# The prompt's attention with stationary values and streaming transposed weights, divided before the transpose

## The chip, the cores and the metric

The kernel runs on one core of a Trainium2 chip. The metric is device time in microseconds (us) of one execution; lower is better. A core has a matrix engine (TensorE, PE in the profile, with its weight loads as PEld), three engines for elementwise work (VectorE as DVE, ScalarE as ACT, GpSimd as POOL), a queue that issues most transfers (SyncE, SP) and 16 DMA engines. Matrix products read SBUF and write to PSUM; VectorE and ScalarE read PSUM.

## The reference

One layer of a streaming encoder runs for two request groups that share weights: one prompt of 256 tokens and eight sampled sequences of 16 tokens. A projection feeds an RWKV-7 recurrence and a sparse attention with 16 heads of 64; both are gated, mixed and projected, and an expert layer (PEER, 16384 experts) follows. The change touches the attention of the prompt, which is, cut to what matters:

```python
def block(args):
    qh, qih, wih, qp = args
    rel = jax.nn.relu(jnp.einsum('bqhd,bsd->bqhs', qih, ki_all))
    score = jnp.einsum('bqh,bqhs->bqs', wih, rel)
    adm = (qp[:, None] // CHUNK) >= k_chunk[None, :]
    score = jnp.where(adm[None], score, -jnp.inf)
    vals, idx = lax.top_k(score, topk)
    ok = vals > -jnp.inf
    ks = gather(k_all, idx)
    vs = gather(v_all, idx)
    s = jnp.einsum('bqhd,bqkhd->bhqk', qh, ks).astype(jnp.float32) * (dh ** -0.5)
    s = jnp.where(ok[:, None], s, -jnp.inf)
    p = jax.nn.softmax(s, axis=-1).astype(vs.dtype)
    return jnp.einsum('bhqk,bqkhd->bqhd', p, vs)
```

For a query, a head's output is the sum over keys of weight times value, with the weights divided by their sum. All data is float32.

## The kernel before

The kernel handles all 384 tokens (128 sampled, 256 of the prompt) in one pass. Its front part, up to about 730 us, is a string of units of five kinds, laid out in program order by the text `ORDER` (line 177): `R` is one pair of heads of the recurrence (`rwkv_pair`, eight of them), `D` one quarter of the attention (`dsa_quarter`, four heads, four of them), `G` a gate projection, `M` a piece of the modulation, `I` the index scores, and `1`, `2`, `3` the choice of keys. The mixing stage (`mix`, L1164) follows; it reads the recurrence's outputs back from memory (`parts`, L1155), and the attention's outputs for its second half. The expert layer takes the rest of the time.

Program order is not the order on the queues. The program is built with a planner, which simulates the units with its own prices, fixes each engine's queue order (so that projections of one unit stand between the steps of another), and hands buffers out as it goes. On the chip every engine runs its queue in order and waits at semaphores.

Projections multiply float32 data that is split in two rounded parts: ScalarE makes the high part `wh` (L230) and VectorE the low part `wl` (L234), and three products are added (tiles `mm<-...`). All matrix products pass the helper `mm` (L226); transposes carry their own lines.

`dsa_quarter` projects queries, keys and values, normalises and rotates them, transposes queries and keys (`qTp`, `kT`), and leaves the values as `vn` (named `vv` in the trace), with tokens on the partitions. Then `attend_s` attends for the sampled tokens and `attend_p` (L1050) for the prompt's. `attend_p` runs over two tiles of 128 queries, i = 0 and 1. Keys are causal by chunks, so tile 0 sees 128 keys and tile 1 sees 256, in `nk` = 1 or 2 pieces. A quarter's four heads are h = 2j + par, where the parity `par` says which half of the partitions holds the head's queries and keys. For a tile:

- the scores of both parities go to two PSUM buffers (L1061), and a matmul with the identity adds the mask (L1066);
- for each parity VectorE takes the maximum (L1068, L1069), and ScalarE the exponentials, with their sums as accumulated output (L1072), into `e` (`se` in the trace);
- for each parity, PE transposes `e` (L1080), VectorE copies the result to `et` (`set`, L1082), and PE multiplies with `et` stationary (128 keys by 128 queries) and 64 columns of values streaming (L1086); queries come out on the partitions, four heads side by side in `pv`;
- VectorE inverts the four sums (L1088) and multiplies `pv` by them into `ob` (L1090);
- PE transposes `ob` twice (L1093), and ScalarE copies the result (L1094) to `obT` (`qr` in the trace), which `dsa_quarter` stores.

The PSUM buffers of all these steps have the tag `dx`, of which there are two. `attend_s` uses the same tag and the same SBUF tags `se` and `set`. The last line of a recurrence pair that matters below is L664, a VectorE product `sq` that L665 stores for the mixing stage; before it stand a chain of normalisation steps (L635 to L652) and a transpose on PE (L663). The serial inverse of a pair (L687, L689) is a chain of 30 short VectorE steps.

Of the kernel before, what the change touches and what calls it, by code (L numbers as in the profile page):

```python
# [17 lines left out]
AF = mybir.ActivationFunctionType  # L18
OP = mybir.AluOpType
# [176 lines left out]
class K:  # L196
# [853 lines left out]
    def attend_p(self, u, qT, kT, vn, obT):  # L1050
        nc = self.nc
        for i in range(2):
            n = 128 * (i + 1)
            nk = i + 1
            tok = slice(i * 128, (i + 1) * 128)
            sm = self.t([128, 4], tag="asum", bufs=2)
            ps2 = [self.ps([128, 2, 256], tag="dx") for _ in range(2)]
            for j in range(2):
                for par in range(2):
                    pr = slice(64 * par, 64 * par + 64)  # L1060
                    self.mm(ps2[par][:, j, :n], qT[pr, j, tok], kT[pr, j, 128:128 + n], start=(j == 0), stop=False, tp=(64 * par, 0))  # L1061
            es = []
            for par in range(2):
                p = ps2[par]
                for j in range(2):
                    self.mm(p[:, j, :n], self.idb, self.mkp[i][:, :n], start=False, stop=True)  # L1066
                mx = self.t([128, 2], tag="amx", bufs=2)
                nc.vector.tensor_reduce(out=mx, in_=p[:, :, :n], op=OP.max, axis=AX.X)  # L1068
                nc.vector.tensor_scalar(mx, mx, -0.125, None, op0=OP.mult)  # L1069
                e = self.t([128, 2, 256], tag="se", bufs=2)  # L1070
                for j in range(2):
                    nc.scalar.activation(e[:, j, :n], p[:, j, :n], AF.Exp, scale=0.125, bias=mx[:, j:j + 1],  # L1072
                                         accum_out=sm[:, 2 * j + par:2 * j + par + 1])
                es.append(e)
            pv = self.ps([128, 4, 64], tag="dx")
            for par, e in enumerate(es):
                pt = self.ps([128, 2, 2, 128], tag="dx")
                for j in range(2):
                    for kc in range(nk):
                        nc.tensor.transpose(pt[:, j, kc], e[:, j, kc * 128:(kc + 1) * 128], self.ident)  # L1080
                et = self.t([128, 2, 2, 128], tag="set")
                nc.vector.tensor_copy(et[:, :, :nk], pt[:, :, :nk])  # L1082
                for j in range(2):
                    h = 2 * j + par
                    for kc in range(nk):
                        self.mm(pv[:, h], et[:, j, kc], vn[:, 1 + kc, h * 64:(h + 1) * 64],  # L1086
                                start=(kc == 0), stop=(kc == nk - 1))
            nc.vector.reciprocal(sm, sm)  # L1088
            ob = self.t([128, 4, 64], tag="ob")
            nc.vector.tensor_tensor(ob, pv, sm.unsqueeze(2).to_broadcast([128, 4, 64]), op=OP.mult)  # L1090
            p = self.ps([128, 2, 128], tag="dx")
            for c in range(2):
                nc.tensor.transpose(p[:, c], ob[:, 2 * c:2 * c + 2].rearrange("p a b -> p (a b)"), self.ident)  # L1093
            nc.scalar.activation(obT[:, :, 128 + i * 128:128 + (i + 1) * 128], p, AF.Copy)  # L1094

    def attend_s(self, u, qT, kT, vn, obT):

# [648 lines left out]
```

## Time and profile before

| | us |
|---|---|
| median of three runs | 1801.76 |
| lowest, highest | 1797.88, 1802.8 |
| profiled execution | 1796.01 |
| its span, first to last instruction | 1794.1 |
| attention blocks of the prompt, quarter 0 | about 268 to 304 |
| quarter 1 | about 409 to 447 |
| quarter 2 | about 570 to 611 |
| quarter 3 | about 698 to 728 |

The page gives busy time per engine, the span in 40 slices, the chain that ended last and the costliest groups of instructions. A group reads "line engine operation, output <- inputs, shape, count"; for a matmul the shape is the stationary operand (rows*columns), then the moving one (partitions x elements). Durations of PE instructions overlap, since matmuls are pipelined: the price of one in a stream is the distance from its start to the next start. The granted clock of PE is given as a share of full speed. "A <- B" in a view of waits means that A stood idle until B had ended, with the total in us, the number of times and the longest.

### The profile page before, as it was taken

What the parts mean: (1) busy time and instruction counts of PE and PEld (TensorE: products, weight loads), DVE (VectorE), ACT (ScalarE), POOL (GpSimd) and SP (SyncE); (2) the same over time, 40 slices, a digit from 0 to 9 for tenths busy, and PEclk for the clock granted to TensorE, in tenths of its full rate; (3) what the DMA queues carried; (4) which work ended last, traced back from release to release, by engine and by line L of the source; (5) the groups of instructions that cost most, each with busy time, mean ns of one, the idle gap of its engine ahead of it and who ended that gap; (6) DMA issues with size and microseconds to landing.
All of it is one profiled execution on the core that took longest, in us unless ns stands there. A gap on an engine that the chain in (4) does not pass through costs nothing.

```text
span 1794.1 us, 33542 instructions
## 1 busy us (share of the span) xinstructions
PE 1714.5 (96%) x12576; PEld 1420.0 (79%) x12576; DVE 1362.0 (76%) x2945; ACT 703.2 (39%) x1411; POOL 700.5 (39%) x752
## 2 busy tenths in 40 slices
PE   6999899999999999999999989999999999999998
PEld 4987687777878877898888889999967667776656
DVE  3448777777867765445999999899958778887885
ACT  4533343333333333324222264488843333333232
POOL 2432242323423320024054446533356565555641
PEclk7999899999999999999999999999999999999999
DMA  8543652463365364665499989964579999999995
GB/s 298 161 128 96 198 178 63 155 195 97 101 198 158 85 217 151 219 202 166 151 336 333 347 305 370 376 228 164 201 267 373 364 377 379 364 395 345 376 378 182
DMA packets 181082, 434.11 MB, mean 242 GB/s; under 512 B 39348, under 2 KB 78388, under 8 KB 180920
## 3 DMA queue, kind: packets, MB, share of 16 engines
q1 hardware_dynamic: 144056, 297.73, 49.4%
q0 software_dynamic: 36864, 134.23, 20.1%
q8 instruction: 99, 1.62, 0.4%
q14 instruction: 63, 0.52, 0.1%
HBM read 401.65 MB, written 30.24 MB: 241 GB/s over the span
## 4 chain that ended last, share of the span: by engine, by line
PE 67%; DVE 15%; DMA 10%; issue 3%; ACT 2%; POOL 2%; SPq 0%; DVEq 0%; ACTq 0%; POOLq 0%
PE mm L226 24%; PE fx L226 15%; PE dx L226 12%; PE cp L226 8%; PE bx L226 7%; DVE raw L1570 2%; DMA w<-in_pv 2%; DVE wl L234 2%; DVE acc L1580 1%; DMA w<-in_w_ada 1%; DMA raw<-in_pv,pe 1%; DMA w<-in_w_in 1%; DMA w<-in_puT 1%; ACT wh L230 1%; DVE psi L1297 1%
## 5 line engine op out<-in xcount | busy, mean ns | idle before, releaser
L234 DVE TENSOR_TENSOR wl<-w,wh 128x1024 fp32r<-128x1024 f32 (+1 forms) x274 | 343.6, 1259 | 119.6 <-ACT wh L230 58.6
L230 ACT ACTIVATE wh<-w 128x1024 fp32r<-128x1024 f32 (+1 forms) x282 | 295.9, 1054 | 207.5 <-PE mm L226 83.0
L1559 POOL DMA_INDIRECT raw<-in_pu,pe x128 | 154.6, 1208 | 181.1 <-PE dx L226 56.0
L226 PE MATMUL fx<-h2h,wh 128*128 128x256 f32 x736 | 216.1, 294 | 7.5 <-ACT wh L230 4.5
L1559 POOL DMA_INDIRECT raw<-in_pv,pe x128 | 173.0, 1351 | 120.4 <-PE dx L226 44.9
L226 PE MATMUL fx<-h2h,wl 128*128 128x256 f32 x736 | 212.2, 289 | 7.7 <-DVE wl L234 7.4
L226 PE MATMUL fx<-h2l,wh 128*128 128x256 f32 x736 | 209.9, 285 | 0.0
L1580 DVE SCALAR_TENSOR_TENSOR acc<-raw,dots,acc 128x1024 f32<-128x1024 f32 x127 | 165.2, 1301 | 10.3 <-DMA raw<-in_pv,pe 9.1
L1570 DVE SCALAR_TENSOR_TENSOR raw<-raw,sh 128x1024 f32<-128x1024 f32 x128 | 161.8, 1274 | 12.5 <-DMA raw<-in_pu,pe 11.7
L226 PEld LDWEIGHTS fx<-h2h,wh 128*128 128x128 f32 x736 | 140.9, 191 | 12.3 <-ACT wh L230 5.9
L226 PEld LDWEIGHTS fx<-h2h,wl 128*128 128x128 f32 x736 | 140.2, 191 | 10.7 <-DVE wl L234 10.1
L226 PEld LDWEIGHTS fx<-h2l,wh 128*128 128x128 f32 x736 | 141.2, 192 | 2.2 <-issue 1.7
L226 PE MATMUL fx<-h2f,w 128*128 128x256 f32 x576 | 129.9, 387 | 6.0 <-ACT G L1471 3.1
L226 PEld LDWEIGHTS fx<-h2f,w 128*128 128x128 f32 x576 | 111.0, 194 | 23.2 <-ACT G L1471 4.0
L226 PE MATMUL mm<-LTh,wh 128*128 128x384 f32 (+2 forms) x352 | 125.1, 356 | 3.3 <-ACT wh L230 2.7
L226 PE MATMUL mm<-LTh,wl 128*128 128x384 f32 (+2 forms) x352 | 123.3, 350 | 0.6 <-DVE wl L234 0.6
L226 PE MATMUL mm<-LTl,wh 128*128 128x384 f32 (+2 forms) x352 | 122.8, 349 | 0.0
L226 PE MATMUL mm<-wh,LTh 128*128 128x256 f32 x336 | 97.9, 292 | 2.7 <-ACT qx L879 2.7
L226 PE MATMUL mm<-wh,LTl 128*128 128x256 f32 x336 | 97.6, 290 | 0.0
L226 PE MATMUL mm<-wl,LTh 128*128 128x256 f32 x336 | 97.3, 290 | 0.0
L1393 POOL TENSOR_TENSOR G<-G,wg 128x144 f32<-128x144 f32 (+1 forms) x64 | 55.5, 889 | 95.6 <-ACT wg L1390 95.6
L1471 ACT ACTIVATE G<-fx 128x256 f32<-128x256 f32 x76 | 28.8, 383 | 122.8 <-PE fx L226 116.6
(560 smaller groups left out, 4193.2 us busy)
## 6 DMA issues: line engine op xcount, KB each, us to landing
w<-in_puT SPq DMA_DIRECT2D x128, 512.0 KB
w<-in_pv SPq DMA_DIRECT2D x128, 512.0 KB
w<-in_w_in SPq DMA_DIRECT2D x70, 512.0 KB
w<-in_w_ada SPq DMA_DIRECT2D x48, 512.0 KB
cKT<-in_cKT SPq DMA_DIRECT2D x32, 256.0 KB
cV<-in_cV SPq DMA_DIRECT2D x32, 256.0 KB
w<-in_w_pq SPq DMA_DIRECT2D x16, 512.0 KB
d<-wst SPq DMA_DIRECT2D x8, 832.0 KB
```

What stands on the lines that cost most here:

```text
L226: return self.nc.tensor.matmul(out, l, r, start=start, stop=stop, skip_group_check=True, **kw)
L230: self.nc.scalar.activation(hi, src, AF.Copy)
L234: (self.nc.vector if eng == "v" else self.nc.gpsimd).tensor_tensor(lo, src, hi, op=OP.subtract)
L1297: nc.vector.max_index(si[:, half, h, 8:16], sv[:, half, h, 8:16], s2)
L1393: (nc.vector if w is p else nc.gpsimd).tensor_tensor(g, g, w[:, :, c0:c1], op=OP.mult)
L1471: nc.scalar.activation(g, p, AF.Gelu_apprx_tanh)
L1559: d = nc.gpsimd.indirect_dma_start(out=u, out_offset=None, in_=src, in_offset=bass.IndirectOffsetOnAxis(ap=e[:, j:j + 1], axis=0))
L1570: nc.vector.scalar_tensor_tensor(u, u, 1.0, h2, op0=OP.mult, op1=OP.mult, accum_out=dots[:, j:j + 1])
L1580: nc.vector.scalar_tensor_tensor(acc, v, dots[:, j:j + 1], acc, op0=OP.mult, op1=OP.add)
```

## The change

The sums are kept by parity. As soon as a parity's exponentials are there, VectorE inverts its two sums and multiplies the parity's weights by them, in place in `e`, a head at a time. PE transposes the divided weights as before; VectorE's copy of the transposed weights goes back into `e` rather than into `et`. The value products come after the transposes of both parities, with 64 columns of values stationary and 128 columns of transposed weights streaming. The heads of parity 0 and 1 write partitions 0 to 63 and 64 to 127 of `pv` (`tp` gives the place in the array: row 0, column 0 or 64), one behind the other in the queue. `pv` then holds the transposed output, and ScalarE copies it to `obT`. The products L1090, the transposes L1093 and their PSUM buffer are gone.

```diff
-            sm = self.t([128, 4], tag="asum", bufs=2)
+            sm = self.t([128, 2, 2], tag="asum", bufs=2)
...
                     nc.scalar.activation(e[:, j, :n], p[:, j, :n], AF.Exp, scale=0.125, bias=mx[:, j:j + 1],
-                                         accum_out=sm[:, 2 * j + par:2 * j + par + 1])
-                es.append(e)
-            pv = self.ps([128, 4, 64], tag="dx")
-            for par, e in enumerate(es):
+                                         accum_out=sm[:, par, j:j + 1])
+                nc.vector.reciprocal(sm[:, par], sm[:, par])
+                for j in range(2):
+                    nc.vector.tensor_scalar(e[:, j, :n], e[:, j, :n], sm[:, par, j:j + 1], None, op0=OP.mult)
+                es.append(e.rearrange("p j (k q) -> p j k q", k=2))
+            for e in es:
                 pt = self.ps([128, 2, 2, 128], tag="dx")
                 for j in range(2):
                     for kc in range(nk):
-                        nc.tensor.transpose(pt[:, j, kc], e[:, j, kc * 128:(kc + 1) * 128], self.ident)
-                et = self.t([128, 2, 2, 128], tag="set")
-                nc.vector.tensor_copy(et[:, :, :nk], pt[:, :, :nk])
-                for j in range(2):
-                    h = 2 * j + par
-                    for kc in range(nk):
-                        self.mm(pv[:, h], et[:, j, kc], vn[:, 1 + kc, h * 64:(h + 1) * 64],
-                                start=(kc == 0), stop=(kc == nk - 1))
-            nc.vector.reciprocal(sm, sm)
-            ob = self.t([128, 4, 64], tag="ob")
-            nc.vector.tensor_tensor(ob, pv, sm.unsqueeze(2).to_broadcast([128, 4, 64]), op=OP.mult)
-            p = self.ps([128, 2, 128], tag="dx")
-            for c in range(2):
-                nc.tensor.transpose(p[:, c], ob[:, 2 * c:2 * c + 2].rearrange("p a b -> p (a b)"), self.ident)
-            nc.scalar.activation(obT[:, :, 128 + i * 128:128 + (i + 1) * 128], p, AF.Copy)
+                        nc.tensor.transpose(pt[:, j, kc], e[:, j, kc], self.ident)
+                nc.vector.tensor_copy(e[:, :, :nk], pt[:, :, :nk])
+            pv = self.ps([128, 2, 128], tag="dx")
+            for j in range(2):
+                for kc in range(nk):
+                    for par, e in enumerate(es):
+                        h = 2 * j + par
+                        self.mm(pv[64 * par:64 * par + 64, j], vn[:, 1 + kc, h * 64:(h + 1) * 64], e[:, j, kc],
+                                start=(kc == 0), stop=(kc == nk - 1), tp=(0, 64 * par))
+            nc.scalar.activation(obT[:, :, 128 + i * 128:128 + (i + 1) * 128], pv, AF.Copy)
```

## The prediction

> **What bounds the kernel now.** I read the page's head first, for the size of everything, and the chain that ended last.
>
> ```profile
> span 1794.1 us, 33542 instructions
> ...
> PE 1714.5 (96%) x12576; PEld 1420.0 (79%) x12576; DVE 1362.0 (76%) x2945; ACT 703.2 (39%) x1411; POOL 700.5 (39%) x752
> ...
> PE 67%; DVE 15%; DMA 10%; issue 3%; ACT 2%; POOL 2%; SPq 0%; DVEq 0%; ACTq 0%; POOLq 0%
> ```
>
> TensorE (PE) is busy nearly always and carries two thirds of the chain. A share over 1794 us says little about an edit of eight short blocks, though: the prompt's attention runs four times (once a quarter of the heads), each time over two tiles of tokens, i=0 and i=1. So the next view is the busy time of each engine in the stretches where the blocks run (columns: stretch, length, PE, PEld, VectorE, ScalarE, GpSimd, granted PE clock, DMA share, GB/s). The first six are the blocks of quarters 0, 1 and 2, i=0 and i=1 in turn; quarter 3 is taken up below.
>
> ```profile
> 270.00:286.00 16.00, 16.00 (x172) 13.49 (x171) 11.09 (x34) 3.90 (x14) 4.82 (x6) 1.00 0.07 19
> 288.00:305.00 17.00, 17.00 (x180) 13.29 (x179) 13.04 (x42) 8.85 (x24) 0.73 (x1) 1.00 0.35 86
> 410.00:426.00 16.00, 16.00 (x154) 12.70 (x152) 11.92 (x34) 4.51 (x17) 5.91 (x12) 1.00 0.30 78
> 429.00:448.00 19.00, 19.00 (x191) 14.78 (x190) 15.33 (x44) 9.34 (x25) 5.86 (x9) 1.00 0.35 97
> 571.00:588.00 17.00, 17.00 (x199) 14.40 (x199) 16.32 (x61) 7.95 (x22) 1.50 (x3) 1.00 0.34 106
> 590.00:611.00 21.00, 21.00 (x218) 18.57 (x216) 17.89 (x45) 8.08 (x21) 6.61 (x9) 1.00 0.31 84
> ```
>
> PE never stops in these six: projections of other units fill the gaps between the attention's steps. VectorE (DVE) is busy 11.1 of 16 us in the first and 16.3 of 17 in the fifth. The waits of PE from 265 to 615 us, of which these are the first and the last of nine rows, sum to 7.4 us:
>
> ```profile
> PE mm L226 <- ACT qx L879: 1.6, 1, 1.6
> ...
> PE cp L226 <- DVE TN L786: 0.2, 1, 0.2
> ```
>
> PE is the bound there, with VectorE close behind, closest in quarter 2. What a change takes off PE should come off the time; what it puts on VectorE is free only as long as VectorE has slack.
>
> **PE, quarters 0 to 2.** The timeline gives the price of each form from one row's start to the next row's start, since durations overlap. A float32 matmul is two records here, a transpose one.
>
> ```profile
> 274.93 0.39 PE L1080 MATMUL dx<-cfirst,se 128*128 128x128 f32 x2
> 275.15 0.39 PE L226 MATMUL fx<-cfront,ra 128*128 128x2 f32 x3
> ...
> 278.64 0.61 PE L226 MATMUL dx<-vv,set 128*128 128x64 f32 x4
> 279.08 0.39 PE L1080 MATMUL dx<-cfirst,se 128*128 128x128 f32 x2
> ...
> 295.87 1.10 PE L226 MATMUL dx<-vv,set 128*128 128x64 f32 x8
> 296.81 0.61 PE L1080 MATMUL dx<-cfirst,se 128*128 128x128 f32 x4
> ```
>
> Two transposes cost 0.22 us (274.93 to 275.15). The value products of one parity of heads cost 0.44 us at i=0 (four records, 278.64 to 279.08) and 0.94 at i=1 (eight records). The block pays them twice and then transposes the result twice: 2x0.44 + 0.22 = 1.10 us at i=0, 2x0.94 + 0.22 = 2.10 at i=1. The transposes of the weights stay as they are.
>
> The new products load 64 columns of values and stream 128 columns of weights, and two heads write the two halves of the array's columns. The trace has that very shape in the sampled tokens' attention and in the state chain:
>
> ```profile
> 267.41 0.44 PE L226 MATMUL dx<-cfirst,so 128*64 128x128 f32 x4
> 267.78 0.60 PE L226 MATMUL dx<-kT,qTp 64*128 64x128 f32 x3
> ...
> 700.43 0.61 PE L226 MATMUL bx<-W,TTs 128*128 128x64 f32 x4
> 700.97 0.65 PE L226 MATMUL cp<-Sb,NO 128*64 128x128 f32 x6
> 701.55 0.33 PE L226 MATMUL cp<-cQ,MBp 64*64 64x64 f32 x4
> ```
>
> A pair of such matmuls (four records) takes 0.37 us including the step back to another form (267.41 to 267.78). The NO group is a pair and a third one alone: 0.58, so what follows the first pair costs 0.21, for one matmul or for a pair side by side. Stepping into the form costs 0.10: the W group starts 0.54 before it, where its like at 278.64 took 0.44. So i=0 has two pairs, 0.10 + 0.37 + 0.21 = 0.68 us, and i=1 four, 0.10 + 0.37 + 3x0.21 = 1.10. PE saves 0.42 and 1.00: 1.42 us a quarter, **4.3 us** over three quarters. Bounds: 5.9 if stepping in and out costs nothing (0.10 and 0.37 - 0.21 = 0.16 in each of six blocks, 1.6), and about nothing if the halves don't run side by side (a rival below).
>
> **VectorE, all quarters.** The change adds a multiplication of the weights by the inverse sum, four a block with 128 elements a row at i=0 and 256 at i=1, and splits one reciprocal in two; the multiplication of the result (L1090) goes, the copy (L1082) stays.
>
> ```profile
> L561 DVE TENSOR_SCALAR kk<-Xk,cols x8: 401/406/420, 125.5 to 575.8; 128x384 f32<-128x384 f32 x8
> ...
> L448 DVE TENSOR_SCALAR xn<-x,ss x3: 752/754/756, 8.5 to 16.8; 128x1024 f32<-128x1024 f32 x3
> ...
> L1088 DVE RECIPROCAL asum<-asum x8: 165/173/179, 275.3 to 716.7; 128x4 f32<-128x4 f32 x8
> ...
> L1090 DVE TENSOR_TENSOR ob<-dx,asum x8: 404/418/425, 283.0 to 723.0; 128x256 f32<-128x256 f32 x8
> ```
>
> The same operation takes 0.406 us for 384 elements and 0.754 for 1024, so 0.00054 us an element: an estimate of 0.27 us for 128 and 0.34 for 256. At i=0 that adds 4x0.27 + 0.17 - 0.42 = 0.83 us, at i=1 4x0.34 + 0.17 - 0.42 = 1.11: 1.94 a quarter, 5.8 over three, 7.8 over four. What hides it is VectorE's slack, 3.1 to 4.9 us in five of the six windows but 0.7 in the fifth (17.00 - 16.32), less than the 0.83 that comes there. Each new reciprocal waits for ScalarE's sums of its parity, and VectorE runs in order: queued behind it are splits (L234), which projections on PE wait for, and the serial inverse (L687, L689), which the recurrence waits for. On PE the products of both parities now wait for the second copy; projections can stand ahead of them. I charge a quarter of the 5.8, **1.5 us**, between nothing and all of it.
>
> The multiplication has a dearer case in the trace:
>
> ```profile
> 705.00 1.00 POOL L650 TENSOR_TENSOR vn<-vn,lnx 128x384 f32<-128x384 f32 x1
> ...
> 705.22 0.82 DVE L636 TENSOR_SCALAR gnm<-gnm 128x6 f32<-128x6 f32 x1
> ...
> L636 DVE TENSOR_SCALAR gnm<-gnm x8: 168/717/993, 280.0 to 705.2; 128x6 f32<-128x6 f32 x8
> ```
>
> Six elements a row need 0.17 us, but 0.82 here: the instruction ends with the GpSimd one beside it. So 0.8 us is the extra for one that meets such an operation. GpSimd is busy 25.4 of 106 us in the six windows; if a quarter of the 24 new multiplications there pay half of 0.8, VectorE gets 2.4 us more. The Trainium skill speaks against the change at this point: "SBUF — State Buffer", section "Who interferes with whom", has a `tensor_scalar` in a two-port mode and a GpSimd instruction block each other for the whole instruction. The rows above agree. I take nothing for it, since the weights become ready where GpSimd mostly rests, and keep it for the range.
>
> **Quarter 3** is another case: the fill has run out, and PE's clock is halved.
>
> ```profile
> 709.50:726.60 17.10, 15.50 (x52) 11.88 (x52) 7.50 (x14) 4.13 (x12) 1.04 (x1) 0.50 0.55 191
> ...
> 706.61 0.41 DVE L1082 COPY set<-dx 128x256 f32<-128x256 f32 x1
> ...
> 709.53 0.38 ACT L1094 ACTIVATE qr<-dx 128x256 f32<-128x256 f32 x1
> ...
> 711.60 2.07 PE L226 MATMUL dx<-kT,qTp 64*128 64x256 f32 x4
> ...
> 714.26 0.69 DVE L1068 TENSOR_REDUCE amx<-dx 128x2 f32<-128x512 f32 x1 [1.13 <-PE dx L226]
> 714.95 0.56 DVE L664 TENSOR_TENSOR sq<-sq,bx 128x384 f32<-128x384 f32 x1
> ```
>
> The last recurrence output (sq, L664) goes to memory and back before the mixing stage can start. It waits on VectorE behind the maximum of i=1 (L1068), which waits for scores, which need the PSUM buffer that i=0 frees with L1094, 2.5 us after the end of its last copy. In the new form two pairs (0.68) and the same ScalarE copy follow that copy, so the buffer is free about 1.6 us sooner. Against it, a reciprocal and two multiplications of i=1 (0.17 + 2x0.34 = 0.85 us) become ready about when L664 does and may stand ahead of it. Between -1.6 and +0.9 I take **-0.5 us**. The PE time that i=1 saves there is hidden: PE waits for the mixing stage's input anyway. ScalarE and the DMA queues get the same instructions as before, and the longer life of the weights' buffer ends before the next tile's scores have a PSUM buffer.
>
> **The sum:** -4.3 + 1.5 - 0.5 = -3.3 us. The profiled execution took 1796.0 us (span 1794.1 and 1.9 around it), so 1792.7; the median of the runs shown, 1801.76, is 5.75 above it, and on that footing the forecast is **1798.5 us**. About 0.3%, 5.4 us, is what a measurement of this kernel can tell from no change; the forecast lies inside it.
>
> **Rivals.**
> - *PE's whole gain arrives.* The slack hides VectorE's additions, and quarter 3 gains its 1.6: -5.9 us, 1790 profiled, 1795.9 as a median, faster by 0.33%. For it: PE's few waits in the rows above. Against it: the fifth window.
> - *VectorE ends the attention stretches.* Its 7.8 us go onto the path in all four quarters, and PE's saving turns into waiting: 1803.8 profiled, 1809.6 as a median, slower by 0.43%. It decides where the slack of a window falls below the 0.8 to 1.1 us added there. For it: the fifth window, and the 2.4 us that GpSimd may add. Against it: five windows with 3 us or more.
> - *The clock falls one step sooner.* In quarter 3 the clock is 0.50 for 17.1 us, and less PE work ahead of it makes the dip longer. Elsewhere a lone dip lasts 3.4 us:
>
> ```profile
> 511.50:514.90 3.40, 3.40 (x13) 3.40 (x12) 2.85 (x5) 2.83 (x4) 0.00 (x0) 0.50 1.08 327
> ```
>
>   One more such step at half speed costs up to 1.7 us: 1794.4, or 1800 as a median, within 0.3%. The Trainium skill, "TensorE: Matmul & The Clock Gate", part 1, has the gate decide in free-running windows of about 3.4 us by how busy PE was. The dips of 3.4 and of five times 3.4 us agree.
> - *The halves don't run side by side.* Then a matmul costs 0.21 alone, i=0 needs 4x0.21 + 0.26 = 1.10 and i=1 8x0.21 + 0.26 = 1.94: PE saves 0.16 a quarter, VectorE's charge stays, and the time is about 1.0 us above before, 1797 or 1803. Against it: the NO group, where a pair costs no more than about one.
>
> **How the numbers follow.** The forecast has 0.40, PE's whole gain 0.28, VectorE as the bound 0.16, the clock 0.06, the halves 0.04. The last 0.06 is for a changed order of the queues, which a planner writes out anew from its own prices; it is split evenly to both sides. So faster by over 0.3% has 0.28 + 0.03 = 0.31, within 0.40 + 0.06 + 0.04 = 0.50, slower 0.16 + 0.03 = 0.19. The range reaches past PE's whole gain with the 5.9 us bound and on the profiled footing (1796.0 - 5.9 - 1.6 = 1788.5, rounded up), and on the other side nearly to VectorE's price: 1789 to 1808.
>
> **What would show it.** Value products from 128*64 weights, in groups of 0.58 and 1.00 us with the step out; no L1090 and no transposes of ob; the added multiplications at 0.27 and 0.34 us, or stretched where GpSimd works beside them. PE's waits from 265 to 615 us stay near 7 us if the slack hides them, and grow by the rival's price, with the new lines of VectorE as releasers, if not. The forecast is wrong if the attention stretches get longer, if a multiplication costs 0.5 us or more without GpSimd beside it, or if the order of units around the blocks changes.

## The result and the profile after

| | before | after |
|---|---|---|
| median, us | 1801.42 (4 runs) | 1815.46 (4 runs) |
| lowest, highest | 1797.88, 1802.8 | 1809.2, 1817.87 |
| profiled execution, its span | 1796.01, 1794.1 | 1809.2, 1807.2 |
| ratio, 95% interval | | 1.0062 (1.0033 to 1.0092) |

The changed kernel is slower by 0.6% (by the medians 14 us, 0.8%), and its median lies above the forecast of 1798.5 and above the range (1789 to 1808). The page of the changed kernel answers the head shown of before:

```profile
span 1807.2 us, 33569 instructions
...
PE 1715.5 (95%) x12560; PEld 1415.8 (78%) x12560; DVE 1370.2 (76%) x2977; ACT 703.2 (39%) x1411; POOL 708.4 (39%) x752
```

TensorE's busy sum is 1.0 us up in a span that is 13.1 longer. (This page's chain covers only the last 2% of the span, so it says nothing here.) The groups of instructions that are new, from the changed kernel's view of groups by shape between 260 and 740 us and its answers on two lines (durations are minimum, median and maximum in ns), and the timeline of value products, read from start to next start:

```profile
L226 PE MATMUL dx<-se,vv 128*64 128x128 f32 x96 | 10.4, 287 | 0.4 <-DVE se L1083 0.4
L1082 PE MATMUL dx<-cfirst,se 128*128 128x128 f32 x48 | 9.5, 282 | 0.2 <-DVE se L1076 0.2
L1076 DVE TENSOR_SCALAR se<-se,asum 128x256 f32<-128x256 f32 x16 | 6.0, 418 | 0.1
L1076 DVE TENSOR_SCALAR se<-se,asum 128x128 f32<-128x128 f32 x16 | 3.8, 280 | 0.1
```

```profile
L1076 DVE TENSOR_SCALAR se<-se,asum x32: 272/310/999, 273.7 to 713.1; 128x128 f32<-128x128 f32 x16, 128x256 f32<-128x256 f32 x16
...
L1074 DVE RECIPROCAL asum<-asum x16: 143/157/166, 272.4 to 712.6; 128x2 f32<-128x2 f32 x16
```

```profile
281.71 0.43 PE L226 MATMUL dx<-se,vv 128*64 128x128 f32 x2
282.07 0.70 PE L226 MATMUL fx<-ARs,kk 64*128 64x256 f32 x2
...
283.01 0.65 PE L226 MATMUL dx<-se,vv 128*64 128x128 f32 x6
283.59 1.13 PE L226 MATMUL dx<-kT,qTp 64*128 64x256 f32 x4
...
300.31 1.09 PE L226 MATMUL dx<-se,vv 128*64 128x128 f32 x16
301.34 0.55 PE L623 MATMUL fx<-cfirst,kk 128*128 128x128 f32 x3
```

The parts of the change have the prices of the prediction. From its start to the next row a block of i=1 takes 1.03 us (300.31 to 301.34; forecast 1.00 on this measure, with 0.10 more for the step into the form ahead of it), one of i=0 0.36 + 0.58 because it is split in two (forecast 0.58 in one piece). A multiplication takes 0.28 us at i=0 and 0.42 on average at i=1, where two are stretched up to 1.00 (forecast 0.27 and 0.34), a reciprocal 0.16. And the new waits are small: TensorE waited 0.2 us for the divided weights in the whole front. Its waits from 265 to 615 us, first and last of seven rows, sum to 5.7 us where before had 7.4:

```profile
PE cp L226 <- DVE Sb L786: 2.2, 2, 1.2
...
PE cp L226 <- DVE NX L773: 0.2, 1, 0.2
```

So 13 us were lost, and these views don't show them in the blocks. One table by stretch, for before and then for after (the columns are those of the prediction's windows: stretch, length, PE, PEld, VectorE, ScalarE, GpSimd, granted clock, DMA share, GB/s):

```profile
690.00:740.00 50.00, 47.44 (x410) 38.78 (x410) 28.52 (x66) 15.81 (x36) 4.17 (x4) 0.83 0.59 198
740.00:840.00 100.00, 97.53 (x616) 91.36 (x614) 46.93 (x63) 34.70 (x44) 23.72 (x22) 1.00 0.52 164
840.00:1062.00 222.00, 209.21 (x1094) 181.76 (x1095) 215.62 (x826) 69.12 (x129) 89.31 (x83) 0.97 0.82 293
```

```profile
690.00:740.00 50.00, 37.37 (x408) 28.83 (x408) 25.87 (x72) 15.26 (x40) 4.16 (x4) 0.90 0.51 176
740.00:840.00 100.00, 98.50 (x607) 92.45 (x606) 46.54 (x61) 33.82 (x41) 19.77 (x17) 1.00 0.53 165
840.00:1062.00 222.00, 202.53 (x1030) 174.74 (x1029) 211.46 (x817) 65.54 (x119) 94.92 (x87) 0.95 0.80 288
```

TensorE stands idle 10 us more between 690 and 740 us, at the junction of the front and the mixing stage, and 7 us more between 840 and 1062, in the scores and the choice of experts, where the program holds nothing of the change. How late one trace is in the front says less. e4 and e6 below hold the kernel before's program up to 690 us, and matched instructions of theirs between 650 and 700 us start 5.5 and 3.8 us later than before's; the changed kernel, e3, e5 and e12 share their front, and start between 1.5 us earlier and 11.1 later. What TensorE waits for at the junction is in the timelines. Before (TensorE, then SyncE's queue):

```profile
714.01 0.85 PE L663 MATMUL bx<-cfirst,y 128*128 128x128 f32 x3
714.65 1.06 PE L1080 MATMUL dx<-cfirst,se 128*128 128x128 f32 x4
...
722.11 1.01 PE L226 MATMUL mm<-pbh,wh 128*128 128x384 f32 x2
...
715.53 0.33 SPq L665 DMA_DIRECT2D d<-sq  x1
717.60 0.80 SPq L1160 DMA_DIRECT2D px<-d  x2
```

After:

```profile
722.20 0.52 PE L663 MATMUL bx<-cfirst,y 128*128 128x128 f32 x3 [3.51 <-DVE y L652]
729.72 1.01 PE L226 MATMUL mm<-pbh,wh 128*128 128x384 f32 x2 [7.00 <-DMA px<-d]
...
718.25 0.33 SPq L961 DMA_DIRECT2D d<-qr  x1
...
723.41 0.32 SPq L665 DMA_DIRECT2D d<-sq  x1
725.40 0.80 SPq L1157 DMA_DIRECT2D px<-d  x2
```

Before, the last recurrence pair (L663) goes ahead of the last attention block's transposes and products, which fill the 8.1 us from there to the first product that needs its output back from memory (`mm<-pbh`). After, the planner has put the whole last quarter of attention ahead of the last pair, and nothing is left to stand in the 7.5 us (722.20 to 729.72). The same comparison for all queues shows how far the planner went: of the 14,800 instructions outside the blocks, which are the same program in both kernels, 1202 of TensorE's queue stand in another place relative to the rest in the front and 144 in the tail, and 279 and 315 of VectorE's.

### The profile page after: what moved, and what is told of

Read it like the earlier page. It is cut to its first block, busy times and chain, and to the rows that moved or that the text cites. A ratio compares the mean times of both kernels' runs of the same rounds, so it can differ in the third digit from the quotient of the medians.

```text
span 1807.2 us, 33569 instructions
## 1 busy us (share of the span) xinstructions
PE 1715.5 (95%) x12560; PEld 1415.8 (78%) x12560; DVE 1370.2 (76%) x2977; ACT 703.2 (39%) x1411; POOL 708.4 (39%) x752
## 5 line engine op out<-in xcount | busy, mean ns | idle before, releaser
L234 DVE TENSOR_TENSOR wl<-w,wh 128x1024 fp32r<-128x1024 f32 (+1 forms) x274 | 344.6, 1264 | 120.2 <-ACT wh L230 65.5
L1556 POOL DMA_INDIRECT raw<-in_pu,pe x128 | 163.7, 1279 | 160.0 <-PE dx L226 52.5
L226 PEld LDWEIGHTS mm<-LTh,wh 128*128 128x128 f32 (+2 forms) x352 | 66.6, 189 | 9.7 <-issue 4.5
```

The lines of the kernel that those rows point to most:

```text
L226: return self.nc.tensor.matmul(out, l, r, start=start, stop=stop, skip_group_check=True, **kw)
L234: (self.nc.vector if eng == "v" else self.nc.gpsimd).tensor_tensor(lo, src, hi, op=OP.subtract)
L1556: d = nc.gpsimd.indirect_dma_start(out=u, out_offset=None, in_=src, in_offset=bass.IndirectOffsetOnAxis(ap=e[:, j:j + 1], axis=0))
```

## The experiments

The theory after these traces: the change's own instructions cost about what was forecast, and the planner's new queue order costs the rest. The rival: the change itself, its divisions and later products, costs it. Both the order and the instructions can be exchanged. A kernel with a fixed order carries a list for each engine, and each instruction is tied to the one ahead of it in its list, without a semaphore; the planner then has to follow (old instructions that the change replaces give their places to the new ones):

```diff
+    info = mybir.DependencyInfo(mybir.DependencyClass.NoSync, mybir.DependencyReason.DATA)
+    for q in QUEUE_LISTS.values():
+        prev = None
+        for n in np.frombuffer(zlib.decompress(base64.b85decode(q)), np.uint16).tolist():
+            if prev is not None:
+                tc.add_manual_dep(by[n], prev.name, info, reason="order")
+            prev = by[n]
```

All sixteen runs are in this table; the ratio is to the kernel before, run beside it (its medians there were 1800.92 to 1803.37).

| run | instructions | queue order | median us | ratio, 95% interval |
|---|---|---|---|---|
| e1 | after | before's | 1802.96 | 1.0009 (0.9988 to 1.0029) |
| e2 | before | after's, outside the blocks | 1821.34 | 1.0138 (1.0095 to 1.0180) |
| e3 | after | own front, before's tail | 1813.03 | 1.0058 (1.0035 to 1.0081) |
| e4 | before | own front, after's tail | 1813.95 | 1.0050 (1.0029 to 1.0070) |
| e5 | after | own, before's at the junction | 1814.46 | 1.0072 (1.0048 to 1.0096) |
| e6 | before | own, after's at the junction | 1819.06 | 1.0095 (1.0059 to 1.0130) |
| e7 | before, a reciprocal split | planner's | 1815.23 | 1.0077 (1.0050 to 1.0104) |
| e8 | before, two heads swapped | planner's | 1824.12 | 1.0116 (1.0082 to 1.0150) |
| e9 | after without division | planner's | 1798.03 | 0.9997 (0.9973 to 1.0022) |
| e10 | after without division | before's | 1800.64 | 0.9998 (0.9979 to 1.0017) |
| e11 | before, division ahead | before's | 1811.20 | 1.0041 (1.0021 to 1.0061) |
| e12 | after | own front up to the junction, then before's | 1808.81 | 1.0041 (1.0009 to 1.0073) |
| e13 | after, two heads swapped | planner's | 1805.85 | 1.0017 (0.9999 to 1.0034) |
| e14 | after, products by head | planner's | 1821.68 | 1.0103 (1.0066 to 1.0141) |
| e15 | after, products by parity | planner's | 1825.70 | 1.0121 (1.0079 to 1.0163) |
| e16 | after, one multiplication for two | planner's | 1810.46 | 1.0025 (0.9998 to 1.0052) |

**Order or mechanism: e1 to e4.** The edit is the one above, with the lists named in the table.

> The changed kernel's instructions, but each engine's queue in the order that the kernel before has (the new instructions of the attention blocks stand where the ones that they replace stood, the division ahead of its transposes). Theory 'order': the change's own instructions cost about the -3.3 us of the prediction and the new queue order the rest, so 1798 us (1794 to 1803). Rival 'mechanism': VectorE's added multiplications and the later products themselves cost it, so this stays at the changed kernel's 1815 us (1809 to 1818).

> The kernel before's instructions, nothing of the change in it, but the 14,800 instructions outside the prompt's attention blocks stand in the queues in the changed kernel's order. 'Order': slow without the change, 1815 to 1820 us (the 14 us that the change costs and the 3.3 that its instructions save). 'Mechanism': 1801 us (1797 to 1805).

> The changed kernel with its own order in the front and, from the first instruction of the mixing stage on (about 735 us), the kernel before's queue order. In the two traces about 7 of the 13 us were there by 735 us, the rest came between 845 and 1050 us. 'Order': the tail's 6 us go, 1809 us (1805 to 1812). 'Mechanism': the tail holds the same instructions in both kernels, so what comes late from the front stays, and the tail's part stays as well: 1815 us (1811 to 1818).

> The kernel before with its own front, and from the mixing stage on the changed kernel's queue order: nothing of the change in it but half of the new order. 'Order': 1801 + 6 = 1807 us (1804 to 1811). 'Mechanism': 1801 us (1797 to 1804).

The rival falls on e1 and e2 together: all of the change in the old order stands at the kernel before's time, +1.6 us (-2.2 to +5.2, the interval times 1802), and none of it in the new order costs as much as the whole change or more: 25 us by the ratio, 19 by the medians, since one run of 1843.76 us weighs on the ratio. The new front (in e3, with the change's own instructions) and the new tail (in e4) each cost by themselves, about 10 and 9 us. e3 was expected 4 us lower and e4 7: taking the old tail alone shows no gain over the changed kernel, though the two intervals leave room for the 6 us expected, and the two parts don't simply add up. Two things weren't separated. The planner hands out buffers as it goes, so an order comes with its buffers. And no run ties the kernel before to its own list; e1 and e10 below, which are tied and at its time, speak against a price of the ties.

**One place in the order: e5 and e6.** The lists are a kernel's own, except between the start of the last quarter's attention and the first instructions of the mixing stage.

> The changed kernel in its own queue order, but at the junction of the front and the mixing stage in the kernel before's: the last recurrence pair's group norm, transposes and store stand ahead of the last quarter's attention again, and the loads of px ahead of the store of qr. Some 20 of the 14,800 instructions outside the blocks change their place. Theory 'junction': this one exchange uncovers the way of the last pair's output through memory (PE idle 3.51 + 7.00 us in the changed kernel against none of over 0.9 us before), so 7 to 8 us come back: 1807 us (1804 to 1811). Rival 'spread': the loss lies in the other displaced places (1202 of PE's queue), 1814 us (1812 to 1818).

> The kernel before in its own queue order, but at the junction in the changed kernel's: six instructions and the last quarter's attention change places, nothing else. 'Junction': 1801.5 + 8 = 1809 us (1806 to 1813). 'Spread': 1802 us (1799 to 1804).

With those of the tail counted, ten instructions and the last quarter's blocks change places in e6, some thirty in e5. e6 costs 17 us; its trace has the changed kernel's waits at the junction (view of waits, 690 to 745 us; the columns are total, times, longest), and a clock of 0.71 there in place of 0.83 (view by stretch):

```profile
PE mm L226 <- DMA px<-d: 6.8, 1, 6.8
PE bx L663 <- DVE y L652: 2.8, 1, 2.8
```

```profile
690.00:740.00 50.00, 39.66 (x375) 29.08 (x375) 19.93 (x58) 11.48 (x34) 4.16 (x4) 0.71 0.28 94
```

e6 lies above its expected range as well (1806 to 1813). But e5, the other way, gives nothing back. The long waits are gone from it, and others and a lower clock have come in their place:

```profile
PE mm L226 <- ACT pbh L230: 2.1, 2, 1.1
PE dx L1082 <- DVE se L1076: 1.9, 2, 1.4
```

```profile
690.00:740.00 50.00, 43.59 (x441) 33.08 (x440) 26.82 (x72) 15.39 (x40) 4.17 (x4) 0.80 0.50 162
```

So the junction can cost this much, and yet taking it away doesn't make the changed kernel faster. The time did not hang on the wait that was easiest to see in the trace alone.

**A change that means nothing: e7 and e8.** Two neutral edits of the kernel before, with the planner free:

```diff
-            nc.vector.reciprocal(sm, sm)
+            nc.vector.reciprocal(sm[:, 0:2], sm[:, 0:2])
+            nc.vector.reciprocal(sm[:, 2:4], sm[:, 2:4])
```

```diff
-                for par in range(2):
+                for par in (1, 0):
```

> The kernel before with a change that means nothing: each block's reciprocal of four sums is made in two halves, 8 instructions of about 0.16 us more, on VectorE. The planner is free; it moves 291 instructions of PE's front queue against the kernel before (the change moves 1202), but it puts the last quarter's attention and the store of qr ahead of the first px, as in the changed kernel. 'Junction': 1809 us (1805 to 1813). 'Spread': in proportion to what is displaced, a quarter of 14 us and the 1.3 of the instructions at most: 1803 to 1806 us.

> The kernel before with the score products of the two heads of a pair issued in the other order: the same instructions. The planner, free, moves 1437 instructions of PE's front queue, more than the change does, but keeps the last pair ahead of the last quarter's attention. 'Junction': 1802 us (1798 to 1806). 'Spread': as much displaced as by the change, 1812 us (1808 to 1818).

Both lie above the ranges of both theories. e7, with the changed kernel's junction, costs 14 us; e8 keeps the good junction, has the same instructions, and costs 21 us, so the junction alone can't be the answer. This is the experiment to remember: exchanging two independent matmul groups of equal size costs at least as much as the change under study (the two intervals overlap a little).

**The parts of the change: e9 to e12.** e11's edit on the kernel before is the division of the diff, with `ob` a copy:

```diff
+                nc.vector.reciprocal(sm[:, par], sm[:, par])
+                for j in range(2):
+                    nc.vector.tensor_scalar(e[:, j, :n], e[:, j, :n], sm[:, par, j:j + 1], None, op0=OP.mult)
...
-            nc.vector.reciprocal(sm, sm)
-            nc.vector.tensor_tensor(ob, pv, sm.unsqueeze(2).to_broadcast([128, 4, 64]), op=OP.mult)
+            nc.vector.tensor_copy(ob, pv)
```

> The changed kernel without any division: no reciprocal and no multiplication by it, the values stationary, the weights not divided (its output for the prompt is left undivided). The planner is free, and keeps the last recurrence pair ahead of the last quarter's attention. Less work for TensorE and for VectorE than in the kernel before. Theory 'the kernel before has a good order, others cost 9 to 21 us': 1797 + 9 or more, 1806 to 1818 us in spite of less work. Rival 'few places': with the junction as before, near the 1797 us (1793 to 1802) of less work.

> The same instructions as the run before this one (values stationary, nothing divided), in the kernel before's queue order. By the prediction's terms: TensorE's -4.3 us and no multiplications, 1796 to 1797 us (1793 to 1800). If the later products cost what the shorter ones save: 1801 us.

> The other part alone, in the kernel before's queue order: the weights divided ahead of their transposes, the products with the transposed weights stationary as before, and ob a copy. By the prediction's terms VectorE's charge without TensorE's gain: 1.5 us of 7.8 on the path, 1803 us (1800 to 1806). If all of VectorE's time is on the path: 1809 us.

> The changed kernel in its own order up to the last quarter's attention (about 690 us), from there on (junction and tail) in the kernel before's. Together with the runs of tail alone and junction alone it says which stretch of the order costs. 'Few places' (junction and tail): the front costs nothing, 1802 us (1798 to 1805). 'Others cost': the displaced 1188 instructions of PE's front queue cost by themselves, 1808 us or more.

e9 refutes "others cost 9 to 21 us": the planner wrote another order for the same instructions as e10 (633 of TensorE's front queue displaced against before) and it is as good, 0.9997 beside 0.9998. A new order may cost nothing. e10's -4.8 us and e11's +1.5 were both expected too low: -0.4 us (-3.8 to +3.1) and +7.4 (3.8 to 11). In e12 the changed kernel's front, with its instructions, costs 7.4 us (1.6 to 13).

**One order of many: e13 to e16.** What was open is whether any order for the changed instructions is slow. Three neutral edits of the changed kernel and one that joins two multiplications:

```diff
-                for par in range(2):
+                for par in (1, 0):
...
-                for kc in range(nk):
-                    for par, e in enumerate(es):
+                for par, e in enumerate(es):
+                    for kc in range(nk):
...
-            for j in range(2):
-                for kc in range(nk):
-                    for par, e in enumerate(es):
+            for par, e in enumerate(es):
+                for j in range(2):
+                    for kc in range(nk):
...
-                for j in range(2):
-                    nc.vector.tensor_scalar(e[:, j, :n], e[:, j, :n], sm[:, par, j:j + 1], None, op0=OP.mult)
+                nc.vector.tensor_tensor(e[:, :, :n], e[:, :, :n], sm[:, par].unsqueeze(2).to_broadcast([128, 2, n]), op=OP.mult)
```

> The changed kernel with the score products of the two heads issued in the other order; the same instructions. The planner moves 1250 instructions of PE's front queue against the changed kernel, but leaves the tail as there (3 of PE's moved) and the junction as there. 'One order of many': anything between 1798 and 1822 us; with the slow junction and the slow tail, 1810 us or more. 'Any order for these instructions': 1815 us (1811 to 1819).

> The changed kernel with the two halves of a head's sum issued one after the other (j, head, half in place of j, half, head); the same instructions. The planner leaves the front nearly as in the changed kernel (146 moved) and writes the kernel before's tail (2 of PE's moved). If the tail's order is worth the 9 us that it cost by itself: 1806 us (1802 to 1811). 'Any order for these instructions': 1815 us (1811 to 1819).

> The changed kernel with the products of one head of each pair ahead of those of the other, so that the first wait for only one copy of transposed weights; the same instructions. The planner writes another front (927 moved against the kernel before), the kernel before's junction and nearly its tail (19 moved). 'One order of many': good places, 1798 us (1793 to 1804), the prediction's own number. 'Any order for these instructions': 1815 us (1811 to 1819).

> The changed kernel with one multiplication for the two sums of a block's head pair in place of two: 16 instructions fewer on VectorE. The planner writes the kernel before's junction and nearly its tail (4 of PE's moved), and a front of its own (1191 moved). 'One order of many': 1798 us (1793 to 1805). 'Any order for these instructions': 1813 us (1809 to 1818).

The changed arithmetic runs in 1806 to 1826 us, depending on an edit that means nothing, so the 14 us don't belong to it. Over the orders that the planner wrote, the changed kernel and e13 to e16 average a ratio of 1.0066; the kernel before, e7 and e8 average 1.0064. My two landmarks failed both ways as predictors of the whole time: e13, with the changed kernel's tail and a last quarter that waits 6.9 us for px, is the fastest; e14 and e15, with the kernel before's tail (e15's nearly), are the slowest and above both of their expected ranges. e15 has the kernel before's junction too, where its first product waits 2.6 us; its trace is 31 us late before it comes there (matched instructions, 650 to 700 us). e16, with the old junction and nearly the old tail, does lie near the kernel before. (First view e13's waits from 690 to 745 us, second e15's first two rows from 690 to 790, since its junction comes at 744 to 753 us.)

```profile
PE mm L226 <- DMA px<-d: 6.9, 1, 6.9
```

```profile
PE dx L1082 <- DVE se L1076: 2.7, 2, 2.2
PE mm L226 <- ACT pbh L230: 2.6, 1, 2.6
```

One part of the loss does repeat from trace to trace. From 800 to 840 us on to 950 to 1062, matched instructions of the five kernels with the changed kernel's tail (the changed kernel, e2, e4, e5, e13) fall back by 5.0 to 5.6 us against before, those of the other twelve by -0.8 to +1.0. Among the waits from 840 to 1062 us is one of TensorE's transposes for the chosen experts' indices (`pix`), first in the changed kernel, then before:

```profile
PE dx L1360 <- DVE pix L1341: 4.3, 1, 4.3
```

```profile
PE dx L1363 <- DVE pix L1344: 0.9, 1, 0.9
```

So the new tail costs about 5 us where it stands, of the 13 between the two traces. That it decides the time of a whole execution isn't shown: e13 has this loss, and e3, without it, is not clearly faster than the changed kernel.

No version is faster than the kernel before beyond its interval; e9 and e10, at its time, leave the division out.

## Why the prediction was wrong

- **The step that failed** is the last part of the chances: "The last 0.06 is for a changed order of the queues, which a planner writes out anew from its own prices; it is split evenly to both sides." The sum was made as if the rest of the program kept its places. It did not, as the prediction's last sign of being wrong had it ("if the order of units around the blocks changes"), and the planner's order is worth from nothing (e9 beside e10) to 21 us (e8), several times the 3.3 us that the sum argued about. Being even on both sides was wrong as well: of eight orders that the planner wrote after an edit, none is faster than the kernel before, and seven lie above it by 0.2 to 1.2% (after, e7, e8, e13 to e16; the intervals of e13 and e16 reach 1).
- **TensorE's -4.3 us**: the prices were right. In e1, the old order, the timeline shows a whole group at i=0 and one at i=1:

```profile
281.44 0.66 PE L226 MATMUL dx<-se,vv 128*64 128x128 f32 x8
282.03 0.70 PE L226 MATMUL fx<-ARs,kk 64*128 64x256 f32 x2
...
298.76 1.09 PE L226 MATMUL dx<-se,vv 128*64 128x128 f32 x16
299.79 0.55 PE L623 MATMUL fx<-cfirst,Xk 128*128 128x128 f32 x3
```

  That is 0.59 and 1.03 us with the step out, as the forecast had it (0.58 and 1.00). The halves run side by side, so that rival is out. As a time the 4.3 us are not to be seen: products without division in the old order (e10) are at -0.4 us (-3.8 to +3.1). TensorE's waits from 265 to 615 us sum to 6.0 us in e10's trace, less than before's 7.4, so no wait there took them, and its trace gains 3.5 us on before's from 250 us to 700, which the spread of single traces could make as well. What became of the 4.3 stays open.
- **VectorE's charge of 1.5 us** was too small, for the old order in which it was reckoned. In e1 TensorE's transposes wait for the divided weights; the first two rows of that kernel's waits from 265 to 615 us:

```profile
PE dx L1082 <- DVE se L1076: 4.4, 4, 1.3
PE mm L226 <- ACT qx L879: 1.6, 1, 1.6
```

  4.4 us in four waits, against 1.5 charged for the same three quarters: as much as TensorE's 4.3. That these two make up e1's +1.6 us (-2.2 to +5.2) is likely but not shown, since e10 has no such waits and doesn't show the 4.3 either; the forecast's -3.3 lies just outside e1's interval. It was not the slack in a window that decided, as the prediction had it, but the place in the queues. In one wait (430 us) the division itself is what TensorE waits for. In the other three the exponentials had ended 0.8 to 1.0 us before the reciprocal, which stood behind other instructions in VectorE's queue: before the wait at 436 us behind a split (L234), where ScalarE was done with the exponentials at 434.5 (e1's timeline of VectorE):

```profile
433.97 1.21 DVE L234 TENSOR_TENSOR wl<-w,wh 128x1024 fp32r<-128x1024 f32 x1
...
435.32 0.15 DVE L1074 RECIPROCAL asum<-asum 128x2 f32<-128x2 f32 x1
```

  The prediction had the splits wait behind the division; here it is the other way round. The changed kernel's own order hides all but 0.2 us of this. That makes the rival "VectorE ends the attention stretches" wrong for the changed kernel, and it is by luck that its 1809.6 us came near the measured time. Division alone in the old order (e11, +7.4) has the size of that rival's 7.8, but its trace shows only 1.5 us of waits for the divided weights from 265 to 615 us.
- **Meeting GpSimd**: two of the 32 multiplications were stretched, at 592.8 and 713.1 us, where GpSimd ran beside them, to 0.86 and 1.00 us in place of 0.34: 1.2 us of VectorE's time in all. Taking nothing for it was about right.
- **Quarter 3's -0.5 us** has no counterpart, since its order around the last pair was exchanged; in e1, which keeps the order, the pair's transposes start 2.1 us after before's 714.01, where the same kernel is 1.5 late at 690. That would be about +0.6 with the wrong sign, within the bounds given (matched instructions of the two traces between 650 and 700 us start 1.45 us later in e1), but one trace of each kernel, with the spread told above, can't show a term this small:

```profile
716.10 0.85 PE L663 MATMUL bx<-cfirst,y 128*128 128x128 f32 x3
```

- **The clock** as a rival of one step (0.06, 1800 us) named something that goes with the times, but one step in quarter 3 is not where it lies. The granted clock over all runs has a median of 0.971 in the changed kernel and 0.978 in the kernel before and 0.979 in e1; over the kernels of this study, median clock and median span go together (correlation -0.78). That the clock causes the times was not tried by itself: idle windows lower both. Against it as the whole answer stands e13, which has the changed kernel's low clock (0.9715) and yet a ratio of 1.0017.

What stays open is which displaced instructions cost the changed kernel its 14 us. The order as a whole is shown to (e1 beside after); front, junction and tail each cost something when put alone into another kernel (e12, e6, e4), but undoing one of them gives nothing that the runs can show back (e5, e3). The tail's 5 us are found in every trace that has its order, and no place that I named predicts a new order's whole time (e13 to e15).

## What to carry to other kernels

Where a planner writes the queue order, an edit is measured together with a new order for everything around it: time a neutral edit first (swap two equal steps) for the spread that a new order alone makes, here 0 to 1.2%, and take a gain below it for no gain. To price the edit itself, fix the order and change the instructions, then fix the instructions and change the order. And read a wait at the place where a trace shows it as a suspect only: put it alone into the good kernel and take it alone out of the bad one, since only the second says what is to be won. Look for it in several traces, too: the same front in the same order was up to 11 us late or 1.5 early here.

## What the runs showed of the hardware

Stalls of TensorE can cost more than they last. In the changed kernel a wait of 4.57 us for ScalarE's `G` empties one window of the clock's 3.4 us steps, and the two that follow run at half clock (windows of 944.7 to 958.3 us):

```profile
944.70:948.10 3.40, 3.40 (x18) 2.88 (x16) 3.40 (x9) 0.00 (x0) 1.80 (x3) 1.00 1.02 396
948.10:951.50 3.40, 0.27 (x2) 0.00 (x0) 3.37 (x19) 0.88 (x1) 2.16 (x3) 0.99 0.97 381
951.50:954.90 3.40, 1.96 (x5) 1.60 (x6) 3.40 (x20) 1.67 (x4) 0.94 (x1) 0.50 0.94 364
954.90:958.30 3.40, 3.40 (x10) 2.68 (x9) 3.40 (x19) 0.00 (x0) 1.77 (x2) 0.50 0.78 219
```

Over the traces of all eighteen kernels, each of the 92 full-speed steps in which TensorE was busy for less than 40% was followed by one at half clock; of those with 40 to 60% busy, 79 of 184 were, of those above 80%, 23 of 8225. The Trainium skill, "TensorE: Matmul & The Clock Gate", part 1, says that the clock halves after an idle window and returns after a busy one; the steps agree, and the share at which it turns is what the rows add. Of the 113 half-speed steps with up to 80% busy none was followed by one at full speed. By these shares, as an estimate: a wait of 2 us inside one step leaves it 41% busy, and in something under half of such cases costs up to 1.7 us more in the next (half of 3.4); split over the border of two steps it leaves both about 70% busy, where a halving was rare (35 of 394). This may be part of why equal waits weigh so differently from order to order; no run tries it.
